# Scaled matmul plus addend on one core: one weight transfer, a strided turn, and a store held for 54 copies

## The chip, the cores and the metric

The kernel runs on one core of a Trainium2 chip. The metric is the time of one execution on the device in microseconds (us); the median of several runs is given. The core has five engines that run their own instruction streams and meet through semaphores: TensorE (PE in the profile; PEld is its weight load), VectorE (DVE), ScalarE (ACT), GpSimd (POOL) and SyncE (SP), which here does nothing but issue DMA transfers. Sixteen DMA engines carry the transfers between main memory and the on-chip memory. A name with a q, such as SPq, is the engine's instruction sequencer.

## The reference

```python
def setup_inputs():
    batch, m, k, n = 16, 512, 1024, 768
    ...

def reference(x, weight, scale, add_value):
    return (scale * np.matmul(x, weight) + add_value).astype(np.float32)
```

All arrays are float32, scale is 0.1. The kernel reads 61.87 MB and writes 25.17 MB.

## The kernel before

**Tiles.** The 8192 rows of x are 64 tiles of 128 rows (K = 1024 wide, 4 KB a row); the addend and the output are 64 tiles of 128 rows by 768 columns. Tiles stand in four blocks of 16 (R): partition p of a block holds 16 neighbouring rows, one for each of its tiles, so a transfer of n tiles moves n neighbouring rows a partition.

**Buffers.** `xs` holds 16 tiles of x in float32. `ao` has 32 slots: an addend tile is loaded into its slot, the result replaces it there and is stored from there. The weights, also float32, land in the last eight slots of `ao` before those are needed for addends, and are cast from there to bfloat16 in `w_bf`. `va` (two buffers of four tiles, a "move" each) holds x cast to bfloat16; `xt` holds four tiles of x turned, two halves of two tiles; `mm` has four accumulators for the products.

**How a tile goes through.**
- The movers (`mover`, line 154) are ScalarE and GpSimd. For each move of four tiles each does eight copies (line 167), every copy casting 32 partitions by 1024 elements from `xs` into a 32-partition block of `va`. ScalarE takes row blocks 0 and 2, GpSimd 1 and 3. Each copy adds one to `by_act` or `by_pool`. Before a move they wait for its x (line 159) and until the move two before it has been turned out of the same `va` buffer (line 160).
- VectorE turns (`turn`, line 177; the transpose is line 182): two tiles of a move at a time, pairs of bfloat16 taken as one float32, in blocks of 32 by 32. It needs all eight copies of both movers for that move.
- TensorE (`tensor_engine`, line 222) multiplies a tile in eight steps of 128 along K, each a weight load of x and two matmuls against `w_bf` (columns 0 to 511 and 512 to 767). It begins when both casts of the weights are done. A pair of tiles is one unit: after it, `done` tells VectorE.
- VectorE finishes (`finish`, line 187; line 191): result = scale times product plus addend, two tiles at a time, in place in `ao`; `made` counts tiles. Its order is written out: two casts of the weights, two turns, then by turns finish and turn, pair by pair (`group`, line 195).

**The order of K.** Any order of K serves as long as x and the weights agree. Before, the weights go in as four chunks of 256 rows; partition p holds rows 2p and 2p + 1 of each chunk, so a partition's data are four pieces of two neighbouring rows, 6 KB each. A copy of x takes 64 elements out of each chunk of 256 and puts them side by side for the turn, 16 runs of 64 over four tiles.

**SyncE's order.** All transfers but three small ones are issued by SyncE, one after another, in the order of `STREAM` (line 22), by `sync_engine` (line 95): "w" weights, "x", "a" addends, "o" stores, "pair" part of the stores of tiles 8 and 15, "a+" only adds to a semaphore. The first x tiles (0 to 7) go out before (line 243), the last store (tiles 60 to 63) after (line 257). Before each it waits as needed: an x load for the copies that free its slots (lines 114 and 115; four tiles are free after eight copies of each mover), an addend load for the addends before it and for the store that empties its slots, a store for `made` (line 146). A wait on SyncE holds up all that stands behind it in `STREAM`. GpSimd issues the rest of the stores of tiles 8 and 15 between its moves (line 251).

What stands around the store of tiles 0 to 7: x of tiles 24 to 31, x of tiles 32 to 39, the "a+" entry, the store of tiles 0 to 7, the store of tiles 9 to 14, the pair, addends 32 to 39, x of tiles 40 to 47. The x of tiles 32 to 39 waits for 48 copies of each mover. One entry of `STREAM`, that at index 4 (`SYNC_AT`), is preceded by an alignment of SyncE's instructions.

Of the kernel before, what the change touches and what calls it, by code (L numbers as in the profile page):

```python
# [8 lines left out]
P = 128  # L9
# [7 lines left out]
VA_BUFS = 2  # L17
MOVE = 4
# [1 line left out]
HALF_BLOCK, PAST, SYNC_AT = 64, 4, 4  # L20

STREAM = [
# [5 lines left out]
]  # L28
FIRST, LAST = (0, 8), (60, 4)
PAIR, TURN_AT = slice(8, 16, 7), 2  # L30
BY_SP, BY_POOL = [(122, 6)], [(117, 5), (0, 105), (105, 12)]

# [2 lines left out]
def kernel(  # L35
# [9 lines left out]
    bf16 = mybir.dt.bfloat16  # L45
    fp32 = mybir.dt.float32
# [7 lines left out]
    KC = K // (2 * P)  # L54
    KJ = 2 * KC
# [1 line left out]
    x_v = x_f.rearrange("(g p t) k -> p g t k", p=P, t=R)  # L57
    add_v = add_f.rearrange("(g p t) n -> p g t n", p=P, t=R)
    out_v = out_f.rearrange("(g p t) n -> p g t n", p=P, t=R)
    w_v = weight.rearrange("(c p r) n -> p c (r n)", p=P, r=2)  # L60

    def rows(view, s, n):
        assert s // R == (s + n - 1) // R
        return view[:, s // R, s % R:s % R + n, :]
# [3 lines left out]
    xs = nc.alloc_sbuf_tensor("xs", [P, X_SLOTS, K], fp32).ap()  # L68
    const = ctx.enter_context(tc.tile_pool(name="const", bufs=1))
    ao = const.tile([P, A_SLOTS, N], fp32, name="ao")  # L70
    w_bf = const.tile([P, KJ, N], bf16, name="w_bf")
    va = [const.tile([P, MOVE * KC, 4, 64], bf16, name=f"va{i}") for i in range(VA_BUFS)]
    xt = const.tile([P, XT_TILES, KC, P], fp32, name="xt")
    mm = psum.tile([P, MM_BUFS, 1024], fp32, name="mm")

    w_sem = [tc.alloc_semaphore(f"w{i}") for i in range(2)]
    x_sem = [tc.alloc_semaphore(f"x{i}") for i in range(X_SLOTS // MOVE)]
    a_sem = tc.alloc_semaphore("a")
    o_sem = [tc.alloc_semaphore(f"o{i}") for i in range(2)]
# [1 line left out]
    by_act, by_pool, pool_go, turned, casts, done, made = (  # L81
        tc.alloc_semaphore(name)
        for name in ("by_act", "by_pool", "pool_go", "turned", "casts", "done", "made"))
    TURNED = MOVE * VA_BUFS
    MADE = TURNED + 2 + MM_BUFS - 2
    W_AT = A_SLOTS - KJ

    def slot(t):
        return t % A_SLOTS

    def store_pair(eng, p, n, sem):
        assert PAIR.stop <= R and PAIR.stop <= A_SLOTS
        eng.dma_start(out_v[p:p + n, 0, PAIR, :], ao[p:p + n, PAIR, :]).then_inc(sem, 16)  # L93

    def sync_engine(eng):
        groups, stores, known = 0, [], {}

        def need(sem, value):
            if known.get(sem, 0) < value:
                eng.wait_ge(sem, value)  # L100
                known[sem] = value

        for at, (op, s, n) in enumerate(STREAM):
            if at == SYNC_AT:
                eng.addr_align(HALF_BLOCK, offset=PAST, max_nops=0)
            last = s + n - 1
            if op == "w":
                dst = ao[:, W_AT + s:W_AT + s + n, :].rearrange("p (c r) n -> p c (r n)", r=2)
                move, sem = eng.dma_start(dst, w_v[:, s // 2:(s + n) // 2, :]), w_sem[s // 4]
            elif op == "x":  # L110
                k = s % X_SLOTS
                if last >= X_SLOTS:
                    moved = 8 * (last + 1 - X_SLOTS) // MOVE
                    need(by_act, moved)
                    need(by_pool, moved)
                move = eng.dma_start(xs[:, k:k + n, :], rows(x_v, s, n))  # L116
                sem = x_sem[k // MOVE]
            elif op == "a":
                if groups:
                    need(a_sem, 16 * groups)  # L120
                if last == A_SLOTS - 1:
                    need(casts, KJ)
                if s <= PAIR.start + A_SLOTS <= last:
                    need(pair_sem, 16 * len(BY_SP))
                    need(aside_sem, 16 * len(BY_POOL))
                if s >= A_SLOTS:
                    i = next(j for j, (a, b) in enumerate(stores) if a <= last - 1 - A_SLOTS < a + b)
                    need(o_sem[i % 2], 16 * (i // 2 + 1))
                move = eng.dma_start(ao[:, slot(s):slot(s) + n, :], rows(add_v, s, n))  # L129
                sem = a_sem  # L130
                groups += 1
            elif op == "pair":
                need(made, MADE + last + 1)
                for p, n in BY_SP:
                    store_pair(eng, p, n, pair_sem)
                continue
            elif op == "a+":
                need(a_sem, 16 * groups)
                eng.sem_inc(a_sem, 16 * (n // G - 1))
                groups += n // G - 1  # L140
                continue
            else:
                i = len(stores)
                if i > 1:
                    need(o_sem[i % 2], 16 * (i // 2))
                need(made, MADE + last + 1)
                move = eng.dma_start(rows(out_v, s, n), ao[:, slot(s):slot(s) + n, :])
                sem = o_sem[i % 2]
                stores.append((s, n))
            move.then_inc(sem, 16)  # L150
            if op == "x" and n == 2 * MOVE:
                eng.sem_inc(x_sem[k // MOVE + 1], 16)

    def mover(eng, copy, parity, count, go=None, first=0, turns=T // X_SLOTS):
        if go is None:
            eng.preload_act_table(mybir.ActivationFunctionType.Copy)  # L156
        with eng.Fori(16 * (first + 1), 16 * (first + turns) + 1, 16) as i:  # L157
            for q in range(X_SLOTS // MOVE):
                eng.wait_ge(x_sem[q], i)
                eng.wait_ge(turned, i + (4 * q - 12) if q < 3 else i)  # L160
                if go is not None:
                    eng.sem_inc(go, 1)  # L162
                k = MOVE * q
                src = xs[:, k:k + MOVE, :].rearrange("p i (c b k) -> p (i c) b k", b=4, k=64)
                for a in (parity, parity + 2):
                    for b in range(4):
                        copy(va[q % VA_BUFS][32 * b:32 * b + 32, :, a, :],  # L167
                             src[32 * a:32 * a + 32, :, b, :]).then_inc(count, 1)

    def vector_engine(eng):  # L170
        ao_g = ao.rearrange("p (g t) n -> p g t n", t=G)

        def cast_w(s, n):
            eng.wait_ge(w_sem[s // 4], 16)
            eng.tensor_copy(w_bf[:, s:s + n, :], ao[:, W_AT + s:W_AT + s + n, :]).then_inc(casts, n)  # L175

        def turn(move, half, moves=None):
            if half == 0:
                eng.wait_ge(by_act, moves)
                eng.wait_ge(by_pool, moves)  # L180
            q = 2 * half * KC
            eng.transpose(  # L182
                xt[:, 2 * half:2 * half + 2, :, :].rearrange("p i c m -> p (i c m)"),
                va[move % VA_BUFS][:, q:q + 2 * KC, :, :].bitcast(fp32).rearrange("p c a k -> p (c a k)"),
            ).then_inc(turned, 2)

        def finish(pair, at, products):
            eng.wait_ge(done, products)
            a = ao_g[:, at, 2 * pair:2 * pair + 2, :]
            q = 2 * (pair % 2)  # L190
            eng.scalar_tensor_tensor(  # L191
                a, mm[:, q:q + 2, 0:N], float(scale), a,
                op0=mybir.AluOpType.mult, op1=mybir.AluOpType.add).then_inc(made, 2)

        def group(i, at, last):
            eng.wait_ge(a_sem, i)
            for p in range(4):
                finish(p, at, i + (4 * p - 12) if p < 3 else i)
                if p < 2 or not last:
                    turn(1 if p < 2 else 0, p % 2, i + 8 if p == 2 else i)  # L200

        cast_w(0, 4)
        cast_w(4, 4)
        turn(0, 0, 8)
        turn(0, 1)
        with eng.Fori(16, 2 * T, 16) as i:
            group(i, bass.ds((i // 16 + A_SLOTS // G - 1) % (A_SLOTS // G), 1), False)
        s = slot(T - G) // G
        group(2 * T, slice(s, s + 1), True)
# [31 lines left out]
    s, n = FIRST  # L241
# [14 lines left out]
    s, n = LAST  # L256
# [36 lines left out]
```

## Time and profile before

| what | value |
|---|---|
| three runs, median | 208.56 us (208.39 to 208.87) |
| the profiled execution, its own time | 209.46 us |
| its span, first to last instruction | 207.7 us |
| mean granted TensorE clock | 0.982 |
| TensorE busy | 167.7 us, 81% |
| VectorE busy | 98.0 us, 47% |
| ScalarE, GpSimd busy | 134.7 us, 65%; 137.7 us, 66% |
| mean DMA rate over the span | 419 GB/s |

The profile is one execution. Its page gives busy times by engine, the span in 40 equal slices (a digit is a slice's busy share in tenths), the DMA queues, the chain of work that ended last, groups of instructions by line with their busy time, count, mean duration and the idle time of the engine ahead of them, and the DMA issues with their size and the time from issue to landing. The trace behind it answers further questions: instructions in order of time (start, duration, engine, line, operation, tiles; in brackets the idle time before and what ended it), and busy time in chosen stretches (stretch, length, busy time and number of instructions of PE, PEld, DVE, ACT and POOL, granted clock, DMA share, GB/s). The DMA share is the mean busy share of the 16 DMA engines; a packet's time counts in the stretch in which it starts, so that a short stretch can show over 1.

### The profile page before, as it was taken

To read this page: it belongs to the slowest core of one execution; us is meant where nothing else is said; L and a number is where in the kernel's file an instruction comes from. 1 tells how busy PE (TensorE), PEld (TensorE's weight loads), DVE (VectorE), ACT (ScalarE), POOL (GpSimd) and SP (SyncE) were. 2 spreads that over 40 slices of the span, in tenths; PEclk is the share of its full clock that TensorE was granted. 3 is DMA by queue.
4 is the path that set the end of the run, shared out by engine and by line. 5 is a ranking of instruction groups with operands and counts; after the bars stand their busy time and mean duration, and the time that the engine had idled before them with its cause. 6 is when DMAs were issued, how large, how long until landed. Compare 5 with 4: busy or idle time off the path is not lost.

```text
span 207.7 us, 2223 instructions
## 1 busy us (share of the span) xinstructions
PE 167.7 (81%) x1008; PEld 50.4 (24%) x512; DVE 98.0 (47%) x66; ACT 134.7 (65%) x129; POOL 137.7 (66%) x135
## 2 busy tenths in 40 slices
PE   0000099999999999999999999999999997999800
PEld 0000023333333333333333333323332232333200
DVE  0005525537555555475555553855551934455310
ACT  2049970799999708999997069999990299900000
POOL 0049994799999907999999359999991199910000
PEclk9999999999999999999999999999999999999975
DMA  7999999999999999999999999999999999998983
GB/s 297 410 380 473 417 447 404 454 454 404 404 454 454 404 448 454 380 426 414 445 419 449 407 451 454 404 428 436 445 431 417 423 447 450 454 454 381 447 379 166
DMA packets 4067, 87.04 MB, mean 419 GB/s; under 512 B 476, under 2 KB 476, under 8 KB 1122
## 3 DMA queue, kind: packets, MB, share of 16 engines
q1 hardware_dynamic: 3874, 86.28, 97.1%
q0 software_dynamic: 192, 0.75, 0.9%
q14 instruction: 1, 0.01, 0.0%
HBM read 61.87 MB, written 25.17 MB: 419 GB/s over the span
## 4 chain that ended last, share of the span: by engine, by line
PE 36%; DMA 29%; POOL 18%; ACT 5%; issue 4%; DVE 3%; SPq 0%; POOLq 0%; DVEq 0%; ACTq 0%
PE mm L214 36%; POOL va L167 17%; DMA xs<-in_x_dram 15%; DMA out_dram<-ao 14%; ACT va L167 5%; DVE xt L182 2%; POOL out_dram L93 1%; DVE ao L191 1%; SPq L129 0%; SPq L116 0%; DVEq L180 0%; POOLq L160 0%; POOLq L162 0%; POOLq L157 0%; DVEq L191 0%
## 5 line engine op out<-in xcount | busy, mean ns | idle before, releaser
L214 PE MATMUL mm<-w_bf,xt 128*128 128x256 bf16 (+1 forms) x1008 | 167.7, 327 | 28.6 <-DVE xt L182 27.7
L167 POOL CAST va<-xs 32x1024 bf16<-32x1024 f32 x128 | 135.5, 1059 | 44.8 <-DMA xs<-in_x_dram 37.4
L167 ACT CAST va<-xs 32x1024 bf16<-32x1024 f32 x128 | 133.4, 1043 | 46.0 <-DMA xs<-in_x_dram 43.0
L191 DVE SCALAR_TENSOR_TENSOR ao<-mm,ao 128x1536 f32 (+1 forms) x32 | 56.2, 1757 | 72.8 <-PE mm L214 68.2
L212 PEld LDWEIGHTS <-xt 128*128 128x128 bf16 x512 | 50.4, 98 | 145.4 <-issue 116.2
L182 DVE STREAM_TRANSPOSE xt<-va 128x1024 f32<-128x1024 f32 x32 | 39.5, 1236 | 9.2 <-POOL va L167 7.1
L175 DVE CAST w_bf<-ao 128x3072 bf16<-128x3072 f32 x2 | 4.5, 2251 | 18.2 <-DMA ao<-in_weight_dram 18.2
L156 ACT ACT_TABLE_LOAD x1 | 1.3, 1283 | 1.3 <-SPq L246 1.3
L93 POOL DMA_DIRECT2D out_dram<-ao x3 | 2.0, 662 | 0.0
L274 POOL MEMSET const-float32-0.0<- 128x1 f32 x1 | 0.1, 98 | 0.2 <-issue 0.2
L274 POOL MEMSET const-bfloat16-1.0<- 128x1 bf16 x1 | 0.1, 101 | 0.0
L274 POOL MEMSET const-float32-1.0<- 128x1 f32 x1 | 0.1, 98 | 0.0
L274 POOL MEMSET const-uint8-127<- 128x1 uint8 x1 | 0.1, 98 | 0.0
## 6 DMA issues: line engine op xcount, KB each, us to landing
xs<-in_x_dram SPq DMA_DIRECT2D x7, 4096.0 KB, 22.3
ao<-in_add_value_dram SPq DMA_DIRECT2D x6, 3072.0 KB, 16.1
out_dram<-ao SPq DMA_DIRECT2D x3, 3072.0 KB, 29.1
ao<-in_add_value_dram SPq DMA_DIRECT2D x1, 6144.0 KB, 24.2
out_dram<-ao SPq DMA_DIRECT2D x1, 6144.0 KB, 31.8
out_dram<-ao SPq DMA_DIRECT2D x1, 4608.0 KB, 15.3
xs<-in_x_dram SPq DMA_DIRECT2D x2, 2048.0 KB, 21.0
ao<-in_weight_dram SPq DMA_DIRECT2D x2, 1536.0 KB, 16.9
```

What stands on the lines that cost most here:

```text
L93: eng.dma_start(out_v[p:p + n, 0, PAIR, :], ao[p:p + n, PAIR, :]).then_inc(sem, 16)
L156: eng.preload_act_table(mybir.ActivationFunctionType.Copy)
L167: copy(va[q % VA_BUFS][32 * b:32 * b + 32, :, a, :], src[32 * a:32 * a + 32, :, b, :]).then_inc(count, 1)
L175: eng.tensor_copy(w_bf[:, s:s + n, :], ao[:, W_AT + s:W_AT + s + n, :]).then_inc(casts, n)
L182: eng.transpose(xt[:, 2 * half:2 * half + 2, :, :].rearrange("p i c m -> p (i c m)"), va[move % VA_BUFS][:, q:q + 2 * KC, :, :].bitcast(fp ...
L191: eng.scalar_tensor_tensor(a, mm[:, q:q + 2, 0:N], float(scale), a, op0=mybir.AluOpType.mult, op1=mybir.AluOpType.add).then_inc(made, 2)
L212: eng.ldweights(x_j, tile_position=(0, 0))
L214: m = eng.add_instruction(mybir.InstMatmult(start_tensor_calc=(j == 0), stop_tensor_calc=(j == KJ - 1), tile_size=(P, P), tile_position=(0 ...
L274: nc = _bacc.Bacc("TRN2", target_bir_lowering=False, num_devices=1)
```

## The change

Three things are changed together.

1. The weights come in one transfer with one semaphore. Partition p gets rows 8p to 8p + 7, which lie side by side in main memory, 24 KB a partition. Both casts wait for that one semaphore.
2. The order of K in x follows: a copy now takes a run of 256 neighbouring elements of each of four tiles (K elements 256b to 256b + 255 go to partition block b), and `va` is declared as [tile, row block, 256]. The chunk order that the copies made before is now made by the turn: it reads `va` with a step of four float32 words (16 bytes) between neighbouring elements and writes `xt` in order.
3. `HOLD` names one store, that of tiles 0 to 7. After its wait for `made`, SyncE waits until `by_act` has reached 54 before it issues it.

`STREAM` is one entry shorter, so index 4 is now the x load of tiles 16 to 23.

```diff
 STREAM = [
-    ("w", 0, 4), ("w", 4, 4), ("a", 0, 8),
+    ("w", 0, 8), ("a", 0, 8),
...
+HOLD = {0: 54}
...
-    w_v = weight.rearrange("(c p r) n -> p c (r n)", p=P, r=2)
+    w_v = weight.rearrange("(p r) n -> p r n", r=KJ)
...
-    va = [const.tile([P, MOVE * KC, 4, 64], bf16, name=f"va{i}") for i in range(VA_BUFS)]
+    va = [const.tile([P, MOVE, 4, 2 * P], bf16, name=f"va{i}") for i in range(VA_BUFS)]
...
-    w_sem = [tc.alloc_semaphore(f"w{i}") for i in range(2)]
+    w_sem = tc.alloc_semaphore("w")
...
             if op == "w":
-                dst = ao[:, W_AT + s:W_AT + s + n, :].rearrange("p (c r) n -> p c (r n)", r=2)
-                move, sem = eng.dma_start(dst, w_v[:, s // 2:(s + n) // 2, :]), w_sem[s // 4]
+                move, sem = eng.dma_start(ao[:, W_AT + s:W_AT + s + n, :], w_v[:, s:s + n, :]), w_sem
...
                 need(made, MADE + last + 1)
+                if s in HOLD:
+                    need(by_act, HOLD[s])
                 move = eng.dma_start(rows(out_v, s, n), ao[:, slot(s):slot(s) + n, :])
...
-                src = xs[:, k:k + MOVE, :].rearrange("p i (c b k) -> p (i c) b k", b=4, k=64)
+                src = xs[:, k:k + MOVE, :].rearrange("p i (b k) -> p i b k", b=4)
...
         def cast_w(s, n):
-            eng.wait_ge(w_sem[s // 4], 16)
+            eng.wait_ge(w_sem, 16)
...
-            q = 2 * half * KC
+            i = slice(2 * half, 2 * half + 2)
             eng.transpose(
-                xt[:, 2 * half:2 * half + 2, :, :].rearrange("p i c m -> p (i c m)"),
-                va[move % VA_BUFS][:, q:q + 2 * KC, :, :].bitcast(fp32).rearrange("p c a k -> p (c a k)"),
+                xt[:, i, :, :].rearrange("p i c (a m) -> p i c a m", a=4),
+                va[move % VA_BUFS][:, i, :, :].bitcast(fp32).rearrange("p i a (k c) -> p i c a k", c=KC),
             ).then_inc(turned, 2)
```

## The prediction

> **What bounds the kernel now.** I read the page first: span, DMA by slice, queues, groups.
>
> ```profile
> span 207.7 us, 2223 instructions
> DMA  7999999999999999999999999999999999998983
> GB/s 297 410 380 473 417 447 404 454 454 404 404 454 454 404 448 454 380 426 414 445 419 449 407 451 454 404 428 436 445 431 417 423 447 450 454 454 381 447 379 166
> ...
> q1 hardware_dynamic: 3874, 86.28, 97.1%
> ...
> L167 POOL CAST va<-xs 32x1024 bf16<-32x1024 f32 x128 | 135.5, 1059 | 44.8 <-DMA xs<-in_x_dram 37.4
> L167 ACT CAST va<-xs 32x1024 bf16<-32x1024 f32 x128 | 133.4, 1043 | 46.0 <-DMA xs<-in_x_dram 43.0
> L191 DVE SCALAR_TENSOR_TENSOR ao<-mm,ao 128x1536 f32 (+1 forms) x32 | 56.2, 1757 | 72.8 <-PE mm L214 68.2
> ...
> L182 DVE STREAM_TRANSPOSE xt<-va 128x1024 f32<-128x1024 f32 x32 | 39.5, 1236 | 9.2 <-POOL va L167 7.1
> ```
>
> The 16 DMA engines are busy from the second slice to the last but two, and SyncE's queue alone fills 97.1% of their span. No compute engine comes near: DVE works 98 us by its groups, ScalarE and GpSimd 134 and 136 us, and both of these idle some 45 us, mostly for x. TensorE is the only other candidate, so I looked at how far its results run ahead of the queue at the end. The first fence holds DMA issues with their time to landing, the second SyncE's issues, the third VectorE's instructions; start and duration lead each row of the last two.
>
> ```profile
> out_dram<-ao SPq DMA_DIRECT2D x1, 6144.0 KB, 31.8
> out_dram<-ao SPq DMA_DIRECT2D x1, 4608.0 KB, 15.3
> out_dram<-ao SPq DMA_DIRECT2D x1, 1536.0 KB, 8.3
> ```
>
> ```profile
> 72.76 0.33 SPq L116 DMA_DIRECT2D xs<-in_x_dram  x1
> 73.27 0.82 SPq L147 DMA_DIRECT2D out_dram<-ao  x2
> 74.14 0.38 SPq L93 DMA_DIRECT2D out_dram<-ao  x1
> 96.00 0.36 SPq L129 DMA_DIRECT2D ao<-in_add_value_dram  x1
> 96.49 0.85 SPq L116 DMA_DIRECT2D xs<-in_x_dram  x1
> ...
> 116.38 0.84 SPq L147 DMA_DIRECT2D out_dram<-ao  x2
> ...
> 160.44 27.70 SPq L147 DMA_DIRECT2D out_dram<-ao  x2
> 198.45 0.33 SPq L257 DMA_DIRECT2D out_dram<-ao  x1
> ```
>
> ```profile
> 16.73 2.33 DVE L175 CAST w_bf<-ao 128x3072 bf16<-128x3072 f32 x1 [16.73 <-DMA ao<-in_weight_dram]
> 20.48 2.18 DVE L175 CAST w_bf<-ao 128x3072 bf16<-128x3072 f32 x1 [1.43 <-DMA ao<-in_weight_dram]
> 24.79 2.37 DVE L182 STREAM_TRANSPOSE xt<-va 128x1024 f32<-128x1024 f32 x2 [2.13 <-ACT va L167]
> ...
> 174.02 1.25 DVE L182 STREAM_TRANSPOSE xt<-va 128x1024 f32<-128x1024 f32 x1 [3.39 <-POOL va L167]
> 175.19 1.72 DVE L191 SCALAR_TENSOR_TENSOR ao<-mm,ao 128x1536 f32 x1
> ...
> 186.01 1.76 DVE L191 SCALAR_TENSOR_TENSOR ao<-mm,ao 128x1536 f32<-128x1536 f32 x1 [1.96 <-PE mm L214]
> ...
> 191.21 1.76 DVE L191 SCALAR_TENSOR_TENSOR ao<-mm,ao 128x1536 f32<-128x1536 f32 x1 [2.29 <-PE mm L214]
> 196.41 1.76 DVE L191 SCALAR_TENSOR_TENSOR ao<-mm,ao 128x1536 f32<-128x1536 f32 x1 [3.44 <-PE mm L214]
> ```
>
> The store of tiles 32 to 47 goes out at 160.44 and lands at 192.2. The store of tiles 48 to 59 follows at the end of the row of 27.70 us, near 187.8, as soon as VectorE has finished tile 59 (186.01 + 1.76), and lands at 203.1. So when it is issued the queue still has 4.4 us of work. The last store goes out at 198.45, 4.6 us before 203.1, and lands at 206.75. TensorE's chain can therefore end some 3 us later (4.4 and 4.6, less about 1 us in which a transfer starts, below) before the queue goes dry. **The time is the DMA stream**: an edit counts by what it does to the time a byte takes, or by a hole that it makes in the queue.
>
> **The change part by part.** The sum is made against the profiled execution: span 207.7 us, its own time 209.46 us, so 1.8 us lie around the span. The median of the three runs shown, 208.56, lies 0.9 us under that execution; I carry differences over to the median.
>
> *Weights in one transfer.* Two transfers of 1.5 MB, made of 6 KB pieces (4 a partition), become one of 3 MB in 24 KB pieces, 512 pieces becoming 128. Windows of the weights (13 to 19), the first add tiles, which have 24 KB pieces (20 to 26), and others used below; the last two columns are the DMA share and GB/s.
>
> ```profile
> 0.74:1.74 1.00, 0.00 (x0) 0.00 (x0) 0.00 (x0) 0.40 (x1) 0.00 (x0) 1.00 0.00 0
> 1.74:2.74 1.00, 0.00 (x0) 0.00 (x0) 0.00 (x0) 0.89 (x1) 0.00 (x0) 1.00 1.76 524
> 13.00:19.00 6.00, 0.00 (x0) 0.00 (x0) 2.27 (x1) 5.88 (x6) 5.64 (x5) 1.00 1.01 425
> 20.00:26.00 6.00, 0.00 (x0) 0.00 (x0) 3.39 (x3) 5.85 (x7) 5.75 (x5) 1.00 0.98 422
> 78.00:84.00 6.00, 6.00 (x39) 1.86 (x19) 2.91 (x2) 5.12 (x5) 4.84 (x5) 1.00 0.99 426
> 85.00:87.00 2.00, 2.00 (x15) 0.59 (x6) 1.74 (x1) 1.95 (x3) 1.88 (x3) 1.00 1.37 524
> ...
> 134.00:135.50 1.50, 1.50 (x11) 0.41 (x5) 0.97 (x1) 1.45 (x3) 1.44 (x2) 1.00 1.37 590
> ```
>
> Share over GB/s is the engine time of a byte: 1.01/425 = 2.38e-3 for the 6 KB pieces, 0.98/422 = 2.32e-3 for the 24 KB pieces, 2.3% less. On 3.15 MB at 422/0.98 = 430 GB/s (7.3 us) that is 0.17 us; rounding of the shares allows 0 to 0.35. I take −0.15.
>
> *One semaphore for both casts.* The first cast no longer starts at 16.73, but where the second does, 20.48; the second follows about 2.2 us later. That would end near 24.9, where the first turn starts now (24.79). What held that turn was the copies beside the casts: the first fence is a row of GpSimd's timeline, its first 16 copies; the second, of the tile view, has the minimum, median and maximum of all in ns.
>
> ```profile
> 13.12 20.31 POOL L167 CAST va<-xs 32x1024 bf16<-32x1024 f32 x16 [12.68 <-DMA xs<-in_x_dram]
> ```
>
> ```profile
> L167 POOL CAST va<-xs x128: 1027/1037/2452, 13.1 to 181.6; 32x1024 bf16<-32x1024 f32 x128
> ```
>
> A GpSimd copy that meets a cast is stretched by up to 1.4 us; without two such, the 16 would take 17.5 us, 1.09 each. With no cast at 16.7 GpSimd would end its eighth copy, which the first turn needs, at 13.12 + 8 × 1.09 = 21.9 instead of 24.7; it meets the casts on the way and waits for one or both. So the first turn moves by +0.1 to +2 us; I take +0.2. TensorE starts that much later, and the time does not: it is within the 3 us.
>
> *The turn strided.* The same 1024 elements are read 16 bytes apart instead of side by side, then written in order. No row shows a strided read by VectorE. The nearest row is the turn's own, 1.24 us; that is the lower end, since as many elements pass. The upper end is four times it, 4.94 us, if every element cost what four neighbours do. From the start of a finish to the turn behind it lie 1.67 us (a finish of 1.72 to 1.76 us, the turn starting as it drains), and TensorE needs 5.2 us a pair (186.01, 191.21, 196.41). Up to 5.2 − 1.7 = 3.5 us a turn fits beside TensorE. I take 1.24, by the nearest row, and price 2.5 too: TensorE would start 1.3 us later, and at 174.02, where TensorE stands still for a turn that GpSimd's copies released late, 1.24 us more would be lost, not added to the first, since that wait takes up earlier lateness. The two last stores would go out at 189.0 and 199.7, still ahead of 192.2 and 203.1. So 0 either way.
>
> The Trainium skill's page "SBUF — State Buffer", section "Door 1: The DMA port swizzle", speaks against this edit: SBUF is reached in lines of 16 bytes, and a stream needs two or more hits a line for full rate, so a read that takes a new line for every element would pay. An estimate at half rate would be about 2.5 us a turn; by that rule the sum stays, by the working above, but half of the room beside TensorE is gone. No row here shows it.
>
> *The copies.* Each of L167 still moves 32x1024 elements, in 4 runs of 256 instead of 16 of 64. The rows of 1043 and 1059 ns are my value; a change of 0.1 us a copy either way is 0.8 us in the eight copies ahead of the turn at 174.02, hidden in the same 3 us.
>
> *The hold.* SyncE now waits for 54 ScalarE copies before the store at 73.27. With it wait the store of tiles 9 to 14, the pair's store (74.14), then the add tiles of 96.00 and the x of 96.49. ScalarE has done 48 copies when x goes out at 72.76 and goes on here:
>
> ```profile
> 78.78 34.14 ACT L167 CAST va<-xs 32x1024 bf16<-32x1024 f32 x32 [7.16 <-DMA xs<-in_x_dram]
> ```
>
> ```profile
> xs<-in_x_dram SPq DMA_DIRECT2D x1, 4096.0 KB, 15.8
> out_dram<-ao SPq DMA_DIRECT2D x1, 3072.0 KB, 22.6
> ```
>
> Six copies at 34.14/32 = 1.07 us end at 85.2. The x issued at 72.76 lands at 88.6 (15.8 later), and the store's bytes move only behind it: it lands at 95.9, 7.3 us after the x, which is the 3.15 MB at full rate. Issued at 85.2 the store is still 3.4 us early. Launch shows what an empty queue takes: issue at 0.74, no byte up to 1.74, full share from then. So about 1.0 us; the last store bounds it from above: 8.3 us to landing less 3.7 us for 1.57 MB is 4.6 us, most of it spent behind another store. At 1.0 the hold costs nothing, at 4.6 it leaves a hole of 1.2 us. Then everything behind stands where it stood, because 96.00 and 96.49 are released by the store's landing and by copies.
>
> The other end is below nothing. In 85 to 87, the last two pieces of x on each engine ahead of the store, a byte took 1.37/524 = 2.61e-3, against 0.99/426 = 2.32e-3 before: 12.5% over 2.4 us, 0.30 us lost. If the store waiting in the queue does that, issuing it later could win it back. Against it: ahead of the store of tiles 16 to 23, queued from 116.38 on (134 to 135.5), a byte took 1.37/590 = 2.32e-3. Range −0.3 to +1.2; I take 0, by the launch row.
>
> *Sum.* −0.15 + 0 + 0 + 0 + 0: span 207.55, median **208.4 us**.
>
> **The rivals.**
>
> *The hold wins back the slow tail.* −0.15 − 0.30 gives 208.1, a little more if the slowest engine had more than the mean of it. For it: 85 to 87. Against it: 134 to 135.5.
>
> *The held store comes too late (the slower side).* Place: behind the x that lands at 88.6. It decides once a transfer issued into a draining queue needs over 3.4 us to its first byte, or x comes in sooner by as much; each µs beyond is a µs of all 16 engines idle, and nothing later gives it back. At 4.6 us: 208.4 + 1.2 = 209.6; half of that 209.0. For it: no row shows this latency within a full stream. Against it: launch's 1.0.
>
> *The turn makes VectorE the bound.* From 3.5 us a turn on. At 4.94 a pair takes 6.6 instead of 5.2 us, 1.4 × 30 = 42 us, less the 3 us spare: about 247. At 3.7 it would be some 3 to 4 us. Against it: the same operation, the same elements.
>
> *TensorE's start slips beyond its cover.* +2 us from the casts with +1.2 from a turn at half rate reaches 3 us; the queue would run dry at the end for tenths, 209.0. Against it: the wait at 174.02 takes up part.
>
> **How the numbers follow.** A measurement of this kernel tells about 0.2%, 0.42 us, from no change: under 208.14 is faster, over 208.98 slower. Forecast 0.63, of which 0.10 falls under 208.14, by the upper end of the weights' gain, and 0.04 above; slow tail won back 0.14, all faster; store too late 0.13, turn as the bound 0.04, start beyond cover 0.04, all slower; the remaining 0.02, a change that moves nothing, to same. Faster 0.24, same 0.51, slower 0.25. The range for 8 in 10 runs from 207.9 (both gains, and as much again from the slowest engine) to 209.3 (between the half and the whole hole); the forecast's own is 208.0 to 208.9.
>
> **What would show it right or wrong.** The window of the weights at 2.32e-3 a byte; both casts from near 20.4 on, back to back; the first turn at 24.9 to 27; the row of L182 at 1.24 (or 2.5, which lengthens VectorE's busy time by 40 us without moving the end); the store issued at 85.2 and landing at 95.8; no slice under 9 tenths between 73 and 96. A DMA share near nothing at 87 to 90 means the late store; an L182 over 3.5 us with TensorE idle between pairs means VectorE; share over GB/s of 2.32e-3 in 85 to 87 the tail won back. I am wrong if the time moves by more than 0.9 us without one of these.

## The result, and the profile after

| | median of the runs | profiled execution: time, span |
|---|---|---|
| before | 208.5 us (208.39 to 208.87, 6 runs) | 209.46 us, 207.7 us |
| changed | 209.87 us (209.39 to 210.06, 6 runs) | 209.9 us, 208.1 us |

The ratio is 1.0056, 95% interval 1.0043 to 1.0069: 1.2 us slower where 0.2 us less was forecast, and the median lies outside the range of 207.9 to 209.3.

The two spans are only 0.4 us apart, since the profiled execution of before took 209.46 us, 1.0 more than the median of its six runs. The first experiment below profiled the same kernel again at 208.43 us, with a span of 206.6; that trace is the base of the comparisons from here on.

Page of the changed kernel, the rows that answer to those of before:

```profile
span 208.1 us, 2223 instructions
DMA  8999999999989999999999999989999999998984
...
q1 hardware_dynamic: 3474, 86.28, 96.9%
...
L169 POOL CAST va<-xs 32x1024 bf16<-32x1024 f32 x128 | 135.2, 1056 | 46.1 <-DMA xs<-in_x_dram 38.7
L169 ACT CAST va<-xs 32x1024 bf16<-32x1024 f32 x128 | 133.4, 1043 | 47.0 <-DMA xs<-in_x_dram 42.5
L193 DVE SCALAR_TENSOR_TENSOR ao<-mm,ao 128x1536 f32 (+1 forms) x32 | 56.1, 1754 | 51.5 <-PE mm L216 47.7
L184 DVE STREAM_TRANSPOSE xt<-va 128x1024 f32<-128x1024 f32 x32 | 65.3, 2042 | 4.7 <-POOL va L169 4.7
```

The turn takes 2.04 us instead of 1.24, VectorE 26 us more in all, and still idles over 50 us; the copies are what they were. The stream is about as full as before; two slices in its middle that stood at 9 tenths now stand at 8, and they begin at 57 and 135 us. SyncE's issues and VectorE's instructions (start, duration):

```profile
84.95 0.82 SPq L149 DMA_DIRECT2D out_dram<-ao  x2
85.83 1.14 SPq L94 DMA_DIRECT2D out_dram<-ao  x1
95.48 0.36 SPq L129 DMA_DIRECT2D ao<-in_add_value_dram  x1
96.15 0.96 SPq L116 DMA_DIRECT2D xs<-in_x_dram  x1
...
161.45 28.46 SPq L149 DMA_DIRECT2D out_dram<-ao  x2
200.22 0.33 SPq L259 DMA_DIRECT2D out_dram<-ao  x1
```

```profile
20.21 4.59 DVE L177 CAST w_bf<-ao 128x3072 bf16<-128x3072 f32 x2 [20.21 <-DMA ao<-in_weight_dram]
24.72 3.90 DVE L184 STREAM_TRANSPOSE xt<-va 128x1024 f32<-128x1024 f32 x2
...
175.02 2.02 DVE L184 STREAM_TRANSPOSE xt<-va 128x1024 f32<-128x1024 f32 x1 [2.62 <-POOL va L169]
...
198.18 1.76 DVE L193 SCALAR_TENSOR_TENSOR ao<-mm,ao 128x1536 f32<-128x1536 f32 x1 [3.44 <-PE mm L216]
```

The store of tiles 0 to 7 goes out at 84.95, as worked out, and the addends behind it at 95.48, earlier than before (96.00 in the prediction's trace, 96.30 in that of e1_again): up to there the change gains. The first turn starts where it did. The second half is late: the turn that GpSimd's copies release stands at 175.02, not 174.02 (173.53 in e1_again), and the last store goes out at 200.22, not 198.45 (197.95 in e1_again).

### The profile page after: what moved, and what is told of

Its sections match the earlier page's. It is cut to its first block, busy times and chain, and to the rows that moved or that the text cites. A ratio compares the mean times of both kernels' runs of the same rounds, so it can differ in the third digit from the quotient of the medians.

```text
span 208.1 us, 2223 instructions
## 1 busy us (share of the span) xinstructions
PE 167.6 (81%) x1008; PEld 50.3 (24%) x512; DVE 123.5 (59%) x66; ACT 134.7 (65%) x129; POOL 137.3 (66%) x135
## 4 chain that ended last, share of the span: by engine, by line
PE 41%; DMA 38%; POOL 5%; DVE 4%; issue 4%; ACT 3%; SPq 0%; DVEq 0%; POOLq 0%; ACTq 0%
PE mm L216 41%; DMA xs<-in_x_dram 20%; DMA ao<-in_weight_dram 9%; DMA out_dram<-ao 9%; POOL va L169 4%; ACT va L169 3%; DVE xt L184 3%; DVE ao L193 1%; POOL out_dram L94 1%; DVE w_bf L177 1%; SPq L245 0%; SPq L129 0%; DVEq L208 0%; SPq L101 0%; DVEq L190 0%
## 5 line engine op out<-in xcount | busy, mean ns | idle before, releaser
L214 PEld LDWEIGHTS <-xt 128*128 128x128 bf16 x512 | 50.3, 98 | 147.3 <-issue 115.8
L184 DVE STREAM_TRANSPOSE xt<-va 128x1024 f32<-128x1024 f32 x32 | 65.3, 2042 | 4.7 <-POOL va L169 4.7
```

Source lines behind the costliest of these rows:

```text
L184: eng.transpose(xt[:, i, :, :].rearrange("p i c (a m) -> p i c a m", a=4), va[move % VA_BUFS][:, i, :, :].bitcast(fp32).rearrange("p i a ( ...
L214: eng.ldweights(x_j, tile_position=(0, 0))
```

## The experiments

Theory one, from the trace: the hold changes where the stream loses time, and which DMA engine ends last. Rivals: the turn, 0.8 us longer, laid bare at 175; the weights in one transfer. All ratios are to the kernel before, with 95% intervals.

**The parts one by one.** The kernel before again:

> The kernel before, unchanged, to have its span beside the others on the same chip. Its profiled execution of before took 209.46 us against a median of 208.5, so the span of a usual execution should be near 206.8, not 207.7. All theories: ratio 1.000 (0.999 to 1.001).

Measured: 0.9995 (0.9984 to 1.0006), 208.43 us.

The hold alone, the changed kernel without it, and the weights in one transfer alone in the old order of K:

```diff
 # e2_hold_only, on the kernel before
+HOLD = {0: 54}
                 need(made, MADE + last + 1)
+                if s in HOLD:
+                    need(by_act, HOLD[s])
 # e3_no_hold, on the changed kernel
-HOLD = {0: 54}
+HOLD = {}
 # e4_one_transfer, on the kernel before
-    ("w", 0, 4), ("w", 4, 4), ("a", 0, 8),
+    ("w", 0, 8), ("a", 0, 8),
-    w_sem = [tc.alloc_semaphore(f"w{i}") for i in range(2)]
+    w_sem = [tc.alloc_semaphore("w")]
```

> The kernel before with the hold alone. If the turn is the cause (each turn 0.8 us longer, 2.04 against 1.24, laid bare behind the x of tiles 56 to 59): ratio 1.000, within 0.1%. If the hold is the cause (another mix of transfers from 85 us on, the x of tiles 56 to 59 landing 1 us later): about 1.005. If the weights in one transfer are the cause: 1.000.

> The changed kernel without the hold. Turn as the cause: ratio 1.004 to 1.006, like the change. Hold as the cause: 0.999 to 1.001. Weights in one transfer as the cause: 1.004 to 1.006 too.

> The kernel before with the weights in one transfer and one semaphore, in the old order of K (6 KB pieces, contiguous turn, no hold). Weights in one transfer (late first cast) as the cause: 1.003 or more. Turn or hold as the cause: 1.000, within 0.1%, with the first turn at 24.7 to 26 us.

Measured: hold alone 1.0048 (1.0030 to 1.0067), without it 1.0002 (0.9990 to 1.0013), one transfer 1.0003 (0.9991 to 1.0015). **The hold is the loss**; turn and weights are worth nothing that can be measured, though each turn is 0.8 us longer. SyncE's alignment, which stands one entry further on in e3_no_hold too, costs nothing that can be measured either.

Where the hold loses it is seen in four stretches: the end of the x ahead of the held store, the end of the stores and the loads behind them, the end of the x ahead of the next stores, and the end of the program. The last two columns are DMA share and GB/s. The kernel before (e1_again), then the hold alone, then the changed kernel:

```profile
84.00:87.50 3.50, 3.50 (x23) 1.06 (x11) 1.76 (x1) 3.40 (x5) 3.32 (x4) 1.00 1.01 374
98.00:104.50 6.50, 6.50 (x42) 1.95 (x20) 3.25 (x3) 6.35 (x7) 6.15 (x7) 1.00 1.04 442
132.50:137.00 4.50, 4.50 (x30) 1.37 (x14) 2.11 (x2) 4.40 (x5) 4.26 (x5) 1.00 0.97 419
...
205.00:207.00 2.00, 0.00 (x0) 0.00 (x0) 0.00 (x0) 0.00 (x0) 0.00 (x0) 0.50 0.00 0
```

```profile
84.00:87.50 3.50, 3.50 (x24) 1.00 (x12) 1.21 (x1) 3.40 (x5) 3.32 (x4) 1.00 0.95 407
98.00:104.50 6.50, 6.50 (x42) 1.96 (x20) 4.33 (x4) 6.19 (x6) 6.15 (x7) 1.00 1.03 420
132.50:137.00 4.50, 4.50 (x30) 1.37 (x14) 2.91 (x2) 4.40 (x5) 4.25 (x5) 1.00 0.97 384
...
205.00:207.00 2.00, 0.00 (x0) 0.00 (x0) 0.00 (x0) 0.00 (x0) 0.00 (x0) 0.50 0.16 68
```

```profile
84.00:87.50 3.50, 3.50 (x23) 1.01 (x11) 2.00 (x3) 3.43 (x4) 3.26 (x5) 1.00 0.88 379
98.00:104.50 6.50, 6.45 (x41) 1.96 (x21) 5.17 (x3) 5.95 (x6) 6.16 (x6) 1.00 1.03 421
132.50:137.00 4.50, 4.20 (x26) 1.35 (x14) 3.82 (x3) 4.40 (x5) 4.26 (x5) 1.00 0.99 410
...
205.00:207.00 2.00, 0.00 (x0) 0.00 (x0) 0.00 (x0) 0.00 (x0) 0.00 (x0) 0.50 0.09 37
```

Share over GB/s is again the engine time of a byte, here in units of 1e-3; 2.32 is the full rate. Ahead of the store (84 to 87.5): 2.70 before, 2.33 with the hold, 2.32 in the changed kernel. The slow x pieces are gone, which is worth 14% of 3.5 us, some 0.5 us. Then it is given back: 98 to 104.5 goes from 2.35 to 2.45 in both held kernels (0.3 us), 132.5 to 137 from 2.32 to 2.53 and 2.41 (0.4 and 0.2 us). (98 to 104.5 holds the small stores of tiles 8 and 15 in all three.) So far that is +0.2 us for the hold alone and zero for the changed kernel, in the mean of the 16 engines. The rest is the last row: with no hold no piece starts after 205.0; with it engines are still at work for 0.16 × 2 us × 16 = 5 engine-us (microseconds of one engine), in the changed kernel 3. The same traces from 205.2 to 207.4 us, in 40 slices of 0.055 us, show how many engines these are. A 223 is one piece of 12 KB that starts in that slice; at 2.32 a byte an engine takes 0.46 us for it, eight to nine slices. The hold alone, then the changed kernel:

```profile
GB/s 0 0 223 223 0 223 0 0 0 0 223 0 223 0 223 0 0 0 223 0 223 0 223 0 0 0 0 0 0 0 0 0 0 0 0 0 0 0 0 0
```

```profile
GB/s 0 0 223 223 0 0 0 223 0 0 0 223 0 0 0 0 0 0 0 223 0 0 0 0 0 0 0 0 0 0 0 0 0 0 0 0 0 0 0 0
```

The nine pieces of the hold alone stand in three groups of three, eight to nine slices apart: three engines move three pieces more each and end over a microsecond behind the rest. In the changed kernel it is three engines as well, one with three pieces and two with one. In e1_again all 40 slices are 0. The program ends with the last engine.

**Which of the stores, and how late.** Behind the held store also wait the store of tiles 9 to 14 and the pair. The edits are to `HOLD` in the kernel with the hold alone, or to the order:

```diff
 # e5_hold_second
-HOLD = {0: 54}
+HOLD = {9: 54}
 # e6_hold_pair: the wait stands ahead of the pair's store alone
-HOLD = {0: 54}
+HOLD = {8: 54}
 # e7_hold_49
-HOLD = {0: 54}
+HOLD = {0: 49}
 # e8_pair_first
-    ("o", 0, 8), ("o", 9, 6), ("pair", 8, 8),
+    ("pair", 8, 8), ("o", 0, 8), ("o", 9, 6),
```

> The kernel before with the wait for 54 copies moved one store on: tiles 0 to 7 are stored at 73 us as before, the store of tiles 9 to 14 and the pair's store wait until 85 us. Late store of tiles 0 to 7 as the cause: ratio 1.000, slow x pieces at 85 us as before. Late store of tiles 9 to 14 or late pair as the cause (engines falling apart at 99 to 111 us): 1.004 to 1.006.

> The kernel before with the wait for 54 copies ahead of the pair's store alone; both larger stores go out at 73 us. Late pair as the cause: 1.004 to 1.006. Late store of tiles 0 to 7 or of 9 to 14 as the cause: 1.000.

> The hold with 49 copies for 54: the store of tiles 0 to 7 goes out at 79.9 us, with 8 instead of 3 us of x ahead of it. If what counts is that the store finds less than some 5 us of work ahead of it: 1.000 with slow x pieces at 85 us. If any delay behind 73 us does it: 1.003 to 1.006, with no slow pieces at 85 and some near 135.

> The held kernel (54 copies) with the pair's store issued ahead of the hold, at 73 us. Late pair as the cause: back to 1.000 to 1.001. Late large stores as the cause: 1.004 to 1.006 as with the hold alone.

Measured: 1.0006 (0.9994 to 1.0018), 1.0003 (0.9994 to 1.0012), 0.9999 (0.9990 to 1.0007) and 1.0042 (1.0026 to 1.0057). Of the stores that the hold delays, only that of tiles 0 to 7 matters, neither the one behind it nor the pair; and 12 us of delay (85.2 against 73.2) cost what 6.6 us (79.8) do not.

**From which point.** 52, 56 and 53 copies, and the changed kernel with 52:

```diff
-HOLD = {0: 54}
+HOLD = {0: 52}   # e9_hold_52, and e18_changed_52 on the changed kernel
+HOLD = {0: 56}   # e10_hold_56
+HOLD = {0: 53}   # e17_hold_53
```

> The hold with 52 copies: the store of tiles 0 to 7 goes out near 83.0 us and can reach the DMA engines near 84.0, ahead of the slow x pieces that start at 84.9 to 85.3 in every kernel without a late store. If the point is that the store must be there when the engines take up the last two x pieces: slow pieces at 85, ratio 0.999 to 1.001. If the loss grows with the delay: 1.003.

> The hold with 56 copies: issue near 87.3 us, when the first engines end their x. If the loss is a hole in the queue: about 1 us of hole at 88 to 89, ratio 1.008 or more. If the loss is what 54 showed (no slow pieces at 85, uneven engines from 99 on), it is there too: 1.005 plus the hole, 1.009 to 1.012.

> The kernel before with the hold at 53 copies, issue near 84.1 us, between 52 (no loss) and 54 (loss). If the store must be known to the engines when they take up their last two x pieces near 84.9 to 85.3: about 1 us from issue to the engines makes it just too late or just in time, ratio 1.000 to 1.005, with slow pieces at 85 on all engines where it is 1.000 and on few or none where it is slower.

> The changed kernel, strided turn and single weight transfer included, with 52 copies for 54. If the hold's last two copies are the whole loss: 0.999 to 1.002, with slow pieces at 85 on all engines. If turn or weights add to a hold: 1.003 or more.

| copies waited for | store issued at | ratio |
|---|---|---|
| none | 73.2 | 0.9995 (0.9984 to 1.0006) |
| 49 | 79.8 | 0.9999 (0.9990 to 1.0007) |
| 52 | 83.0 | 1.0005 (0.9992 to 1.0018) |
| 53 | 84.1 | 1.0007 (0.9994 to 1.0020) |
| 54 | 85.2 | 1.0048 (1.0030 to 1.0067) |
| 56 | 87.3 | 1.0126 (1.0110 to 1.0142) |
| 52, changed kernel | 82.7 | 1.0008 (0.9993 to 1.0023) |

The point lies near 84 to 85 us. With 53 its runs spread from 208.24 to 209.19 us, and its median, 208.84, lies between: this one is at the edge. Two copies fewer cure the whole change.

What the store meets there shows in the last two pieces of x on each engine. Each row below holds one piece of 32 KB for each of the 16 engines, first the last but one, then the last: no hold (e1_again), 53, and 54 (the hold alone).

```profile
84.50:85.70 1.20, 1.20 (x9) 0.38 (x4) 0.80 (x1) 1.18 (x2) 1.14 (x2) 1.00 1.39 437
85.70:87.38 1.68, 1.68 (x12) 0.49 (x5) 0.96 (x1) 1.63 (x3) 1.62 (x2) 1.00 0.75 312
```

```profile
84.50:85.70 1.20, 1.20 (x9) 0.36 (x4) 0.00 (x0) 1.18 (x2) 1.14 (x2) 1.00 1.02 437
85.70:87.38 1.68, 1.68 (x13) 0.52 (x6) 1.00 (x1) 1.63 (x3) 1.62 (x2) 1.00 0.86 312
```

```profile
84.50:85.70 1.20, 1.20 (x10) 0.39 (x4) 0.00 (x0) 1.18 (x2) 1.14 (x2) 1.00 1.02 437
85.70:87.38 1.68, 1.68 (x13) 0.49 (x5) 1.09 (x1) 1.63 (x3) 1.62 (x2) 1.00 0.73 312
```

A byte takes 3.18 and 2.40 with no hold, 2.33 and 2.76 with 53, 2.33 and 2.34 with 54. So with the store issued at 84.1 only the last piece is slow, and at 85.2 none is. The execution traced with 53 is the slowest of its runs (209.19 us), and in 205.2 to 207 its share is 0.03, one engine for a microsecond. The four stretches with 52 and with 56:

```profile
84.00:87.50 3.50, 3.50 (x23) 1.07 (x11) 1.76 (x1) 3.40 (x5) 3.32 (x4) 1.00 1.01 374
98.00:104.50 6.50, 6.50 (x41) 1.96 (x20) 3.45 (x3) 6.35 (x7) 6.15 (x7) 1.00 1.04 441
...
205.00:207.00 2.00, 0.00 (x0) 0.00 (x0) 0.00 (x0) 0.00 (x0) 0.00 (x0) 0.50 0.02 6
```

```profile
84.00:87.50 3.50, 3.50 (x24) 1.00 (x12) 1.21 (x1) 3.40 (x5) 3.32 (x4) 1.00 0.91 393
98.00:104.50 6.50, 6.50 (x42) 1.96 (x20) 4.33 (x4) 6.15 (x6) 6.15 (x7) 1.00 1.02 340
```

52 is the kernel before again, slow x pieces (2.70) included; its 0.02 is a piece that starts just after 205, and in 205.2 to 207 its share is 0.00. With 56 a byte takes 3.00 in 98 to 104.5, which is 1.4 us lost there against no hold. That is a dose: 2.35, 2.45, 3.00 for no hold, 54, 56. A hole there is too, but a small one, in the trace of 56 by single microseconds:

```profile
87.00:88.00 1.00, 1.00 (x9) 0.29 (x3) 1.00 (x2) 0.97 (x2) 0.94 (x2) 1.00 0.01 0
88.00:89.00 1.00, 1.00 (x8) 0.29 (x3) 1.00 (x2) 0.98 (x2) 0.94 (x2) 1.00 0.94 393
```

Issued at 87.3, the store's first pieces start after 88.1: in 86.7 to 88.1 the rate is 0. The last pieces of x start by 86.7 and take some 1.2 us each, so an engine stands still for about half a microsecond. With the hold of 54 alone there is no such gap (0.93 and 393 GB/s in 87 to 88).

**Why single engines end late.** The small stores of tiles 8 and 15 are shared out by hand: 6 partitions by SyncE, 122 by GpSimd in three transfers. Without them (tiles 8 to 15 in one store), without and with the hold; all by SyncE, without and with; all by GpSimd with the hold; and another store held instead:

```diff
 # e11_no_pair, e12_no_pair_hold
-    ("o", 9, 6), ("pair", 8, 8),
+    ("o", 8, 8),
-BY_SP, BY_POOL = [(122, 6)], [(117, 5), (0, 105), (105, 12)]
+BY_SP, BY_POOL = [], []
 # e13_sp_small, e14_sp_small_hold
+BY_SP, BY_POOL = [(0, 128)], []
 # e16_pool_small_hold
+BY_SP, BY_POOL = [], [(0, 128)]
 # e15_late_o16
-HOLD = {0: 54}
+HOLD = {16: 92}
```

> The kernel before with tiles 8 to 15 in one store, no small stores of tiles 8 and 15 by SyncE or GpSimd, no hold. A base for the next run: 0.996 to 1.006.

> The same with the hold of 54. If the small stores of tiles 8 and 15 between 99 and 112 us are what makes single engines late in the held kernel: the same as the run without hold, within 0.1%, or 0.2% faster by the slow pieces that are gone at 85. If the slow pieces go elsewhere and fall unevenly with or without small stores: 0.3 to 0.6% over the run without hold.

> The kernel before with the whole store of tiles 8 and 15 by SyncE, 128 partitions in one transfer, none by GpSimd; no hold. A base for the next run: 0.998 to 1.006.

> The same with the hold of 54. If GpSimd's small stores are what makes single engines late in the held kernel: within 0.15% of the run without hold. If small pieces of any queue do: 0.3 to 0.6% over it.

> The held kernel (54) with the small stores of tiles 8 and 15 all by GpSimd in one transfer of 128 partitions, even over the engines. If uneven shares of the small stores are the cause: 0.999 to 1.002. If GpSimd's queue as such is: 1.003 to 1.006.

> The kernel before with another store held: that of tiles 16 to 23 waits for 92 copies, issue near 134.1 instead of 116.3 us, 3 to 4 us ahead of the landing of the x before it, as with 54. If any store that comes that late costs: 1.003 to 1.006. If the cost needs the small stores behind the held one: 0.999 to 1.002.

| small stores | without hold | with 54 |
|---|---|---|
| shared out (as before) | 0.9995 (0.9984 to 1.0006) | 1.0048 (1.0030 to 1.0067) |
| none | 1.0036 (1.0022 to 1.0050) | 1.0046 (1.0032 to 1.0060) |
| all by SyncE | 1.0041 (1.0027 to 1.0054) | 1.0039 (1.0026 to 1.0053) |
| all by GpSimd | not run | 1.0031 (1.0021 to 1.0042) |

This was the surprise. Without the sharing the kernel is slower by as much as the hold costs, and then the hold costs nothing that can be told. The end of e11_no_pair and of e13_sp_small:

```profile
205.00:207.00 2.00, 0.00 (x0) 0.00 (x0) 0.00 (x0) 0.00 (x0) 0.00 (x0) 0.50 0.03 12
```

```profile
205.00:207.00 2.00, 0.00 (x0) 0.00 (x0) 0.00 (x0) 0.00 (x0) 0.00 (x0) 0.50 0.03 12
```

0.03 × 2 × 16 is 1 engine-us, and in 205.2 to 207 the share is still 0.03 in both. The slices of e13_sp_small from 205.2 to 207.4 show two pieces, one behind the other:

```profile
GB/s 0 0 0 223 0 0 0 0 0 0 0 0 223 0 0 0 0 0 0 0 0 0 0 0 0 0 0 0 0 0 0 0 0 0 0 0 0 0 0 0
```

So one engine ends about a microsecond behind the rest. In the kernel before the unequal shares let the engines end together (0.00), and under the hold they no longer do. That it is the same engine which ends late in each of these kernels is not shown. e16 tells less than was hoped: its even shares alone would cost what it lost, as in e13, and it was not run without the hold. Another late store cost nothing: that of tiles 16 to 23, issued at 133.8 instead of 116.3, gave 0.9995 (0.9984 to 1.0007). But it went out 4.0 us before the x ahead of it landed (115.8 + 22.0 = 137.8). With 54 that lead is 3.1 us (72.6 + 15.7 = 88.3, less 85.2) and with 53 4.4 us (72.6 + 15.9 = 88.5, less 84.1), so this run is nearer to the edge than to the loss, and it does not show what a store there costs when it comes later still.

What stays open is why pieces of x ahead of a waiting store run slow at all, why the slow pieces leave 84 to 87.5 when the store comes after 85, why they come back at 98 to 104.5 and 132.5 to 137, and why there on some engines more than on others. The traces show when and where, not what the engines wait for.

## Why the prediction was wrong

- **That the time is the DMA stream** held: 26 us more of VectorE and a later start of TensorE came to 1.0002 (e3_no_hold).
- **Weights, −0.15 us**: the window of the weights (13 to 19) has a share of 1.06 at 459 GB/s, 2.31 for a byte, as forecast, but in the time it is not to be seen. e3_no_hold and e4_one_transfer have intervals of ±0.12%, some ±0.25 us, so the gain is neither shown nor excluded.
- **Casts, first turn +0.1 to +2 us**: the start moved from 24.79 to 24.72, a little below the lower end: it follows the two casts (4.59 us from 20.21) without a wait for a copy.
- **Turn, 1.24 taken, 2.5 priced**: 2.04 us. The size was nearer the upper price, and the cover held as worked out: 65.3 instead of 39.5 us of VectorE cost nothing. The rule of the Trainium skill, "SBUF — State Buffer", section "Door 1: The DMA port swizzle", on reads that take a new 16-byte line for every element pointed the right way: an element costs (2042 − 1236)/1024 = 0.8 ns more, so that the turn takes 1.65 times as long, not twice as in the estimate. It did not decide.
- **The hold, 0 taken, −0.3 to +1.2**: this is the step that failed. "At 1.0 the hold costs nothing" was right on the hole: there is none with 54, and with 56 the first pieces started 0.8 us after the issue (87.3 to 88.1). The slow tail was won back, 0.5 us, as in the rival to which I gave 0.14. But I went on: "everything behind stands where it stood", and that was false. The stream behind the store ran slower at 98 and at 132, which gave the 0.5 us back, and the engines ended apart: three of them over a microsecond behind the rest. The hold alone measured 1.0048, 1.0 us. That this lies within the term's bounds is luck, for the bounds priced a hole, and the mechanism was in no rival: the late-store rival had engines idle at 87 to 90, and the windows show none idle there. The 0.25 that I gave to the slower side stood on three other mechanisms.
- **The base**: I worked on a profile that was 0.9 us slower than its kernel's median. I carried differences over, but did not ask what made that execution longer. Its own trace shows it, from 205.2 to 207.4 us:

```profile
GB/s 0 0 0 0 0 223 0 0 0 0 0 0 0 223 0 0 0 0 0 0 0 0 0 0 0 0 0 0 0 0 0 0 0 0 0 0 0 0 0 0
```

One engine ran two pieces behind the rest, as in e13_sp_small; the lag of a single engine was there to be read. I summed shares and rates over 16 engines, where the end is set by the last one.

## What to carry to other kernels

When the DMA engines are full, the end is set by the latest of 16, not by their mean: before costing an edit that moves transfers about, look at the last two microseconds of the stream, where here a share of 0.03 was a microsecond of one engine and 0.16 three late ones. A store issued "just in time" for a full queue is not free though no hole shows: here it had to go out by some 84 us, about a microsecond before the engines took up the last two pieces of the load ahead of it, and 1 to 2 us decided. It cost something only in the kernels whose small stores were shared out so that the engines end together; in the two variants without that sharing the hold changed nothing that can be told. And when the profiled execution is not near the median, take another as the base before reading tenths of a microsecond from it.

## What was not expected of the hardware

- The last pieces of a load ahead of a queued store ran slow, 2.70 against 2.32 in 84 to 87.5. When the store was queued later they ran at full rate, and others, 14 and 48 us later, slow instead. It is no rule: ahead of the store of tiles 16 to 23, queued 18 us before (116.38), a byte took 2.32 in 134 to 135.5.
- With transfers of 128 partitions alone and none by GpSimd (e13_sp_small) the DMA engines still do not end together: one ends about a microsecond behind the rest, and the ratio is 1.0041.
- A float32 transpose on VectorE that reads every fourth element takes 2042 instead of 1236 ns, 1.65 times as long.
